# Later modulation vectors on POOL, their weight blocks fetched and added behind fixed units of the projection weights

## The chip, the cores and the metric

The kernel runs on one core of a Trainium2 chip. The metric is the device time of one execution in microseconds (us). TensorE (PE, its weight loads PEld), VectorE (DVE), ScalarE (ACT) and GpSimd (POOL) compute; SyncE (SP) issues all transfers (DMA). Each of them takes its instructions in order and waits for semaphores of the others.

## What is computed

Two layers of a diffusion backbone over 512 latent and 256 context tokens of width 1024. Each layer is modulated: from the vectors c and c_ctx come shift, scale and gate, each as silu(c) @ w_ada[l] + b_ada[l].

```python
for l in range(DEPTH):                                   # 2 layers
    shift, scale, gate = jnp.split(jax.nn.silu(c) @ w_ada[l] + b_ada[l], 3, axis=-1)
    shift_c, scale_c, gate_c = jnp.split(jax.nn.silu(c_ctx) @ w_ada[l] + b_ada[l], 3, axis=-1)
    h = rms_norm(x, norm_g[l]) * (1.0 + scale[:, None]) + shift[:, None]
    hc = rms_norm(ctx, norm_g[l]) * (1.0 + scale_c) + shift_c
    ...  # projections of h and hc by w_in[l]; neighbourhood, latent and differential attention
    x_new = x + gate[:, None] * merge_branches(o_na, o_mla, o_diff, z, gm, w_br[l], w_out[l])
    if not last:
        ctx = ctx + gate_c * merge_branches(co_na, co_mla, co_diff, cz, cgm, w_br[l], w_out[l])
    x = x_new
```

## The kernel before

**Units.** Weights of the projections come as units (`unit`, L133): a load of up to 128x384 float32 into one of seven stages (`ws`), a high half by ACT (L122), and a low half (L127) by DVE or, for every second unit without a gain, by POOL; nine buffers each for `wh` and `wl`. `mm3` (L113) multiplies in three passes (lines 115 to 117).

**Steps.** A layer's `mixer` (L867) runs twelve steps in the order D, M, N (differential, latent, neighbourhood heads), four of each. A step projects its heads (eight units in D and N, four with a gain in M), computes a z gate (three units) and some of the 24 `gm` gates (three units each, their count by `NGM`), and computes the attention of the heads of the step before. Step 0 also holds the compressed projections. Then come the branches, the gate (`ada_gate`, L258) and `out_proj` (L1014), which multiplies its result by the gate and, in layer 0, builds the next layer's h. The framework orders each engine's instructions by priorities (`at`, L80) and by a modelled time line; `issue_after` ties the instructions of one engine in a block behind a given one.

**Modulation vectors.** Each w_ada[l] falls into six chunks of 512 columns: 0 and 1 shift, 2 and 3 scale, 4 and 5 gate; each chunk into eight blocks of 128x512 (256 KB). `ada_rows` (L215) multiplies a block by the two columns silu(c) and silu(c_ctx), as one fp32 matmul (two records) per block into a quarter of the partitions of the one PSUM bank `fl`, which zgate and gm also use. DVE copies the bank to rows (L231). For chunks below 4, `ada_ss` (L244) sums the four quarters and turns the row into columns with four small matmuls (L250), and DVE writes A and B (L254). For the gate chunks, eight rows of 512 go to DRAM (`rowsd`, L242), and `ada_gate` loads them (nine rows with the bias) and spreads them over 128 partitions with a matmul (L270). Four chunks of layer 0 are made at the start (`fast`, tile `fs`); the other eight are later ones (`ada_later`, L233; tile `aw`, four buffers), placed by hand after steps 4, 5, 7, 8, 8 and 10 of layer 0 (chunks 4 and 5 of layer 0, four chunks of layer 1) and after steps 4 and 6 of layer 1 (its chunks 4 and 5).

**POOL** also raises mean squares to the power -0.5 (L167), scales softmax rows of N and M heads (L741), applies parts of the rotary tables (L441, L619 to L635), multiplies outputs by z (L778) and adds branches (L981). PSUM has banks of four kinds: `sc` (one pair), `bk` two, `pj` three, `fl` one.

## Time and profile before

| what | value |
|---|---|
| median of 3 runs | 1945.37 us (1943.38 to 1948.09) |
| the profiled execution | 1946.06 us |
| its span, first to last instruction | 1944.3 us |
| mean granted clock of TensorE | 0.993 |
| PE busy | 1882.9 us |
| DVE, ACT, POOL busy | 1213.2, 936.3, 766.0 us |
| moved by DMA | 243.28 MB |

Busy is the time in which an engine had at least one instruction under way. The ends of matmuls are modelled and overlap, so the start of the next matmul tells more of what one costs than its own length. The granted clock is a share of 2.4 GHz; it has two levels, 1.2 and 2.4 GHz, and a value between is a mean over a stretch.

### The profile page before, as it was taken

Reading aid. Unit: us, or ns where it says so; the run is one execution under the profiler, and the core shown is the slowest. Engines: PE = TensorE matmul, PEld = TensorE weight load, DVE = VectorE, ACT = ScalarE, POOL = GpSimd, SP = SyncE. Lnnn points to the kernel's source line nnn. Section 1 sums busy time; section 2 is a strip of 40 time slices with the busy share of each in tenths; the row PEclk is TensorE's granted clock in tenths of the full one; section 3 lists DMA queues with packets and bytes.
Section 4 is the critical chain, followed back from the end, with each engine's and each line's share of the span. In section 5 each row is a group of like instructions: output and inputs, shape, how many; then the busy total and the mean of one; then the engine's idle time right before and its main releaser. Section 6 shows DMA issues by size and latency. Waiting matters only on the chain.

```text
span 1944.3 us, 33969 instructions
## 1 busy us (share of the span) xinstructions
PE 1882.9 (97%) x11650; PEld 1731.5 (89%) x11650; DVE 1213.2 (62%) x2808; ACT 936.3 (48%) x2422; POOL 766.0 (39%) x1057
## 2 busy tenths in 40 slices
PE   7999999999999999999999999999999999999998
PEld 4999999989998988989899988898799699889878
DVE  5557677746774555646664365667668566766763
ACT  4445456535553544445432254555545446555531
POOL 3434243333532332333356364434344334444363
PEclk9999999999999999999999999999999899999999
DMA  9554123343444333332655243422522422442663
GB/s 319 170 176 144 39 66 112 104 130 115 141 122 131 91 107 123 109 105 80 197 179 171 81 142 123 142 71 79 175 62 73 145 75 84 126 128 65 200 187 117
DMA packets 172600, 243.28 MB, mean 125 GB/s; under 512 B 22710, under 2 KB 127560, under 8 KB 172428
## 3 DMA queue, kind: packets, MB, share of 16 engines
q1 hardware_dynamic: 172428, 241.12, 40.1%
q8 instruction: 92, 1.51, 0.3%
q14 instruction: 80, 0.66, 0.1%
HBM read 190.38 MB, written 44.49 MB: 121 GB/s over the span
## 4 chain that ended last, share of the span: by engine, by line
PE 87%; DVE 4%; DMA 4%; ACT 2%; issue 1%; POOL 1%; SPq 0%; DVEq 0%; ACTq 0%; POOLq 0%
PE pj L117 11%; PE pj L115 11%; PE pj L116 11%; PE fl L115 10%; PE fl L116 9%; PE fl L117 9%; PE sc L690 6%; PE bk L851 4%; PE bk L680 4%; PE fl L230 2%; PE bk L810 2%; PE sc L731 1%; DMA aw<-in_w_ada 1%; PE pj L640 1%; PE pj L451 1%
## 5 line engine op out<-in xcount | busy, mean ns | idle before, releaser
L122 ACT CAST w<-ws 128x384 fp32r<-128x384 f32 (+3 forms) x520 | 236.8, 474 | 260.9 <-PE fl L116 146.7
L127 POOL TENSOR_TENSOR w<-ws,w 128x384 fp32r<-128x384 f32 (+3 forms) x260 | 242.8, 940 | 289.9 <-ACT w L122 279.5
L115 PE MATMUL fl<-h,w 128*128 128x384 f32 (+1 forms) x864 | 313.5, 363 | 4.3 <-DVE zs L392 2.2
L115 PE MATMUL pj<-w,h 128*128 128x384 f32 (+2 forms) x944 | 313.9, 335 | 2.0 <-DVE kl L127 1.1
L116 PE MATMUL pj<-w,h 128*128 128x384 f32 (+2 forms) x944 | 309.7, 329 | 1.1 <-POOL w L127 1.1
L117 PE MATMUL fl<-h,w 128*128 128x384 f32 (+1 forms) x864 | 310.1, 359 | 0.0
L116 PE MATMUL fl<-h,w 128*128 128x384 f32 (+1 forms) x864 | 310.1, 359 | 0.0
L117 PE MATMUL pj<-w,h 128*128 128x384 f32 (+2 forms) x944 | 308.5, 331 | 1.2 <-POOL h L127 1.0
L127 DVE TENSOR_TENSOR w<-ws,w 128x384 fp32r<-128x384 f32 (+2 forms) x260 | 177.5, 687 | 65.5 <-ACT w L122 59.4
L167 POOL TENSOR_TENSOR ss<-ss,nhalf 128x4 f32<-128x4 f32 (+1 forms) x144 | 143.6, 998 | 184.6 <-DVE ss L166 165.5
L741 POOL TENSOR_SCALAR P<-P,st 128x512 f32<-128x512 f32 (+1 forms) x128 | 107.9, 846 | 259.2 <-DVE st L737 223.3
L694 ACT ACTIVATE P<-sc,st 128x768 f32<-128x768 f32 (+1 forms) x192 | 159.5, 832 | 101.5 <-DVE st L775 39.0
L117 PEld LDWEIGHTS pj<-w,h 128*128 128x128 f32 x944 | 177.1, 189 | 10.7 <-issue 5.0
L684 DVE TENSOR_TENSOR pt<-bk,pt 128x512 fp32r<-128x512 f32 (+1 forms) x256 | 147.8, 586 | 61.2 <-ACT pt L683 58.6
L115 PEld LDWEIGHTS pj<-w,h 128*128 128x128 f32 x944 | 177.7, 189 | 9.0 <-issue 4.6
L116 PEld LDWEIGHTS pj<-w,h 128*128 128x128 f32 x944 | 178.4, 189 | 4.1 <-issue 2.5
L115 PEld LDWEIGHTS fl<-h,w 128*128 128x128 f32 x864 | 163.0, 189 | 16.1 <-DVE zs L392 3.7
L683 ACT CAST pt<-bk 128x512 fp32r<-128x512 f32 (+1 forms) x256 | 127.2, 506 | 99.1 <-PE bk L680 96.7
L117 PEld LDWEIGHTS fl<-h,w 128*128 128x128 f32 x864 | 162.8, 188 | 12.1 <-DVE w L127 0.6
L116 PEld LDWEIGHTS fl<-h,w 128*128 128x128 f32 x864 | 163.1, 189 | 9.5
L690 PE MATMUL sc<-qk,qk 96*128 96x512 f32 (+3 forms) x592 | 143.5, 337 | 3.8 <-DMA qk<-qk 2.9
L680 PE MATMUL bk<-cst,P 128*128 128x128 f32 x832 | 130.2, 274 | 4.7 <-DVE pt L684 2.4
(237 smaller groups left out, 3978.3 us busy)
## 6 DMA issues: line engine op xcount, KB each, us to landing
ws<-in_w_qkv SPq DMA_DIRECT2D x128, 192.0 KB
ws<-in_w_gm SPq DMA_DIRECT2D x96, 192.0 KB
aw<-in_w_ada SPq DMA_DIRECT2D x64, 256.0 KB
ct<-cqd SPq DMA_DIRECT2D x40, 384.0 KB
ct<-ckd SPq DMA_DIRECT2D x48, 256.0 KB
ws<-in_w_z SPq DMA_DIRECT2D x48, 192.0 KB
thd<-th SPq DMA_DIRECT2D x48, 192.0 KB
ws<-in_w_br SPq DMA_DIRECT2D x48, 192.0 KB
```

The costliest lines, as they stand in the source:

```text
L115: mm(out, a[0], b[0], start=first, stop=False)
L116: mm(out, a[0], b[1], start=False, stop=False)
L117: mm(out, a[1], b[0], start=False, stop=last)
L122: nc.scalar.copy(hi, src)
L127: (nc.gpsimd if le == "g" else nc.vector).tensor_tensor(lo, src, f(hi), ALU.subtract)
L167: nc.gpsimd.tensor_tensor(out, out, self.nhalf[:, :cols], ALU.pow)
L680: nc.tensor.transpose(pt[:, i * P:(i + 1) * P], src[:, (b0 + i) * P:(b0 + i + 1) * P], self.ident)
L683: nc.scalar.copy(h, v)
L684: nc.vector.tensor_tensor(lo, v, f(h), ALU.subtract)
L690: mm(s[:, d0:d0 + w], x, y, start=i == 0, stop=i == len(ops) - 1)
L694: nc.scalar.activation(p, src, AF.Exp, bias=st[:, m:m + 1], accum_out=st[:, 2 + m:3 + m])
L741: nc.gpsimd.tensor_scalar(p, p, st[:, 4 + m:5 + m], 0.0, ALU.mult, ALU.add)
```

## The change

The eight later vectors are no longer matmuls. `ada_later` only puts their 64 blocks on a list, all of a layer's at step 0. From then on `unit` fetches a block behind the load of every third unit, if no more than one is held (`ada_fetch`; two buffers of `aw` in place of four), and when POOL takes the low half of a unit at least two units later, the block is used behind that (`ada_use`). `ada_add` multiplies the block by silu(c) as a scalar per partition and adds it to an accumulator of 128x512 per stream, both on POOL: two streams for layer 0's chunks and for shift and scale, one for layer 1's gate. After the eighth block, chunks below 4 are summed over partitions by eight matmuls with a column of ones; the gate chunks go to DRAM as 128x512 accumulators, and `ada_gate` loads them, adds the bias to their first row and sums over partitions with a matrix of ones. What is left at the end of the steps is drained.

```diff
-ADA = ((4, 5, 7, 8, 8, 10), (4, 6))
...
+        self.ada_todo, self.ada_held, self.nunit = [], [], 0
+    RATE = 3
...
         self.background(self.last)
+        self.ada_fetch(self.last)
...
             self.nsplit += 1
-            self.split(hi[:, :m], lo[:, :m], raw[:, :m], "a", "g" if self.nsplit % self.NS == 0 else "v")
+            le = "g" if self.nsplit % self.NS == 0 else "v"
+            done = self.split(hi[:, :m], lo[:, :m], raw[:, :m], "a", le)
+            if le == "g":
+                self.ada_use(done)
...
+        self.sC = self.cpool.tile([P, KT, 2], F32, name="sC")
+        nc.vector.tensor_scalar(self.sC, th, 0.5, None, ALU.mult)
+        self.sT = pool.tile([P, KT, 32], F32, name="sT")
...
-                st = self.wpool.tile([P, 512], F32, tag="aw", bufs=4, name=self.n("aw"))
-            if self.AFT and not fast:
-                with self.tc.issue_after(self.last.ins):
-                    nc.sync.dma_start(st, w[:, k])
-            else:
-                nc.sync.dma_start(st, w[:, k])
+                raise AssertionError
+            nc.sync.dma_start(st, w[:, k])
             g = 32 * (k % 4)
             nc.tensor.matmul(ps[g:g + 32, :], self.sT[:, k, :], st, start=k < 4, stop=k >= 4, tile_position=(0, g))
         nc.vector.tensor_copy(rows, ps)
 
     def ada_later(self, l, ch, pool):
-        rows = pool.tile([P, 512], F32, tag="th", bufs=1, name=self.n("arow"))
-        self.ada_rows(l, ch, rows, None, False)
+        self.ada_todo += [(l, ch, k, pool) for k in range(KT)]
+
+    def ada_fetch(self, ins):
+        self.nunit += 1
+        if not self.ada_todo or self.nunit % self.RATE or len(self.ada_held) > 1:
+            return
+        l, ch, k, pool = self.ada_todo.pop(0)
+        st = self.wpool.tile([P, 512], F32, tag="aw", bufs=2, name=self.n("aw"))
+        with self.tc.issue_after(ins.ins):
+            self.nc.sync.dma_start(st, self.io["w_ada"][l, ch][:, k])
+        self.ada_held.append((self.nunit, st, l, ch, k, pool))
+
+    def ada_use(self, ins):
+        if not self.ada_held or self.nunit < self.ada_held[0][0] + 2:
+            return
+        _, st, l, ch, k, pool = self.ada_held.pop(0)
+        with self.tc.issue_after(ins.ins):
+            self.ada_add(st, l, ch, k, pool)
+
+    def ada_drain(self):
+        while self.ada_held or self.ada_todo:
+            if not self.ada_held:
+                l, ch, k, pool = self.ada_todo.pop(0)
+                st = self.wpool.tile([P, 512], F32, tag="aw", bufs=2, name=self.n("aw"))
+                self.nc.sync.dma_start(st, self.io["w_ada"][l, ch][:, k])
+                self.ada_held.append((0, st, l, ch, k, pool))
+            _, st, l, ch, k, pool = self.ada_held.pop(0)
+            self.ada_add(st, l, ch, k, pool)
+
+    def ada_add(self, st, l, ch, k, pool):
+        nc = self.nc
+        strs = (0, 1) if l == 0 or ch < 4 else (0,)
+        if k == 0:
+            self.acc = pool.tile([P, 2, 512], F32, tag="acc", bufs=1, name=self.n("acc"))
+        acc = self.acc
+        for s in strs:
+            g = self.sC[:, k, s:s + 1]
+            if k == 0:
+                nc.gpsimd.tensor_scalar(acc[:, s], st, g, 0.0, ALU.mult, ALU.add)
+                continue
+            t = st
+            if s != strs[-1]:
+                t = self.wpool.tile([P, 512], F32, tag="at", bufs=1, name=self.n("at"))
+            nc.gpsimd.tensor_scalar(t, st, g, 0.0, ALU.mult, ALU.add)
+            nc.gpsimd.tensor_tensor(acc[:, s], acc[:, s], t, ALU.add)
+        if k < KT - 1:
+            return
         if ch < 4:
-            self.ada_ss(l, ch, rows, self.fl())
+            pt = self.fl()
+            for i in range(4):
+                for s in strs:
+                    nc.tensor.matmul(pt[:, 2 * i + s:2 * i + s + 1], acc[:, s, i * P:(i + 1) * P], self.ones[:, 0:1], start=True, stop=True)
+            self.ada_put(l, ch, pt)
             return
         if l not in self.rowsd:
-            self.rowsd[l] = self.dram.tile([2, 4, 2, 512], F32, name=f"rowsd{l}")
-        for g in range(4):
-            self.nc.sync.dma_start(self.rowsd[l][ch - 4, g], rows[32 * g:32 * g + 2, :])
+            self.rowsd[l] = self.dram.tile([2, 2, P, 512], F32, name=f"rowsd{l}")
+        for s in strs:
+            nc.sync.dma_start(self.rowsd[l][ch - 4, s], acc[:, s])
 
     def ada_ss(self, l, ch, rows, pt):
...
+        sel = self.cst[:, C_SEL:C_SEL + 2]
+        for i in range(4):
+            self.nc.tensor.matmul(pt[:, 2 * i:2 * i + 2], rows[:, i * P:(i + 1) * P], sel, start=True, stop=True)
+        self.ada_put(l, ch, pt)
+
+    def ada_put(self, l, ch, pt):
...
-        selb = pool.tile([9, 2, P], F32, tag="selb", bufs=1, name=f"selb{l}")
-        nc.sync.dma_start(selb, self.io["selb"])
         for hf in range(2):
-            rows = pool.tile([9, 512], F32, tag="arow", bufs=1, name=self.n("arow"))
-            nc.sync.dma_start(rows[0:8, :], self.rowsd[l][hf].rearrange("g s n -> (g s) n"))
-            nc.sync.dma_start(rows[8:9, :], self.io["b_gate"][l:l + 1, hf * 512:(hf + 1) * 512])
+            bias = pool.tile([1, 512], F32, tag="gbias", bufs=1, name=self.n("gbias"))
+            nc.sync.dma_start(bias, self.io["b_gate"][l:l + 1, hf * 512:(hf + 1) * 512])
             for s in strs:
+                rows = pool.tile([P, 512], F32, tag="arow", bufs=1, name=self.n("arow"))
+                nc.sync.dma_start(rows, self.rowsd[l][hf, s])
+                nc.vector.tensor_tensor(rows[0:1, :], rows[0:1, :], bias, ALU.add)
                 ps = self.bk()
-                nc.tensor.matmul(ps, selb[:, s, :], rows[0:9, :], start=True, stop=True)
+                nc.tensor.matmul(ps, self.ones, rows, start=True, stop=True)
...
-            for _ in range(ADA[l].count(step)):
-                self.at("ada")
-                self.ada_later(*ada.pop(0), pool)
+            if step == 0:
+                while ada:
+                    self.ada_later(*ada.pop(0), pool)
             self.base += self.PRI["step"]
+        self.ada_drain()
```

The constant `selb` goes, the padded `sT` moves into the pool of the start, and `ada_put` is the rest of the old `ada_ss`.

## Rows read from the trace of the kernel before

**Rows 1.** The page, busy us (share of the span) xinstructions of each engine.

```profile
PE 1882.9 (97%) x11650; PEld 1731.5 (89%) x11650; DVE 1213.2 (62%) x2808; ACT 936.3 (48%) x2422; POOL 766.0 (39%) x1057
```

**Rows 2.** Waits of PE and PEld: waiter, releaser, us in total, times, longest.

```profile
PE fl L230 <- DMA aw<-in_w_ada: 5.8, 5, 3.2
PE pj L451 <- DVE qn L445: 5.3, 5, 1.3
...
PE pj L116 <- POOL w L127: 1.1, 1, 1.1
...
PEld bk L680 <- POOL P L741: 2.7, 3, 1.2
```

**Rows 3.** Groups by form, whole span: busy us, mean ns, idle before.

```profile
L230 PE MATMUL fl<-aw,sT 128*32 128x512 f32 x128 | 40.5, 626 | 5.9 <-DMA aw<-in_w_ada 5.8 <-DVE qn L445 0.2
```

**Rows 4.** Timeline of PE, 477 to 487: start us, us, instruction, count.

```profile
477.07 1.07 PE L230 MATMUL fl<-aw,sT 128*32 128x512 f32 x8
...
484.94 0.34 PE L117 MATMUL pj<-w,h 128*128 128x384 f32 x1
485.21 1.05 PE L230 MATMUL fl<-aw,sT 128*32 128x512 f32 x2
486.19 0.45 PE L115 MATMUL pj<-w,h 128*128 128x384 f32 x1
486.47 0.33 PE L116 MATMUL pj<-w,h 128*128 128x384 f32 x1
```

**Rows 5.** Windows: us, PE, PEld, DVE, ACT, POOL busy, clock, DMA share, GB/s.

```profile
1507.00:1525.00 18.00, 13.58 (x59) 7.73 (x60) 7.40 (x20) 5.85 (x17) 2.38 (x4) 0.72 0.44 131
```

**Rows 6.** Timeline of the same stretch, SP's fetches and PE's wait.

```profile
1509.37 1.83 SPq L228 DMA_DIRECT2D aw<-in_w_ada  x4
...
1514.11 1.91 PE L230 MATMUL fl<-aw,sT 128*32 128x512 f32 x2 [3.15 <-DMA aw<-in_w_ada]
```

**Rows 7.** The chain of waits, start: start us, us, what.

```profile
24.33 1.07 PE fl L250 x8
```

**Rows 8.** Timeline near the end, layer 1's second gate rows.

```profile
1893.59 0.29 SPq L266 DMA_DIRECT2D arow<-rowsd  x1
...
1899.48 1.12 PE L270 MATMUL bk<-arow,selb 9*128 9x512 f32 x2 [0.66 <-DMA arow<-rowsd]
```

**Rows 9.** Groups by form of POOL, 128x512 multiply and add.

```profile
L741 POOL TENSOR_SCALAR P<-P,st 128x512 f32<-128x512 f32 x64 | 49.3, 775 | 73.0 <-DVE st L737 69.2 <-PE bk L720 2.7 <-PE bk L680 0.8
...
L981 POOL TENSOR_TENSOR yf<-yf,tht 128x512 f32<-128x512 f32 x16 | 24.0, 1509 | 6.8 <-DVE tht L980 6.7
```

**Rows 10.** Windows of the two stretches, columns as in rows 5.

```profile
122.00:840.00 718.00, 706.88 (x4555) 668.25 (x4554) 456.82 (x1120) 360.78 (x968) 250.48 (x363) 1.00 0.38 114
1190.00:1400.00 210.00, 200.68 (x1220) 177.12 (x1219) 145.17 (x361) 115.23 (x301) 89.56 (x134) 0.99 0.39 116
```

**Rows 11.** The same windows, POOL busy with L167 alone.

```profile
122.00:840.00 718.00, 64.73 (x62) 1.00 0.38 114
1190.00:1400.00 210.00, 23.65 (x25) 0.99 0.39 116
```

**Rows 12.** The same windows, POOL busy with L741 alone.

```profile
122.00:840.00 718.00, 40.24 (x48) 1.00 0.38 114
1190.00:1400.00 210.00, 13.60 (x16) 0.99 0.39 116
```

**Rows 13.** Waits of SP's queue: waiter, releaser, total, times, longest.

```profile
SPq L228 <- PE fl L230: 57.7, 31, 9.2
```

**Rows 14.** Timeline of DVE splits, POOL idle (1507) and working (1893).

```profile
1507.06 0.55 DVE L127 TENSOR_TENSOR w<-ws,w 128x384 fp32r<-128x384 f32 x1
...
1893.31 1.20 POOL L127 TENSOR_TENSOR w<-ws,w 128x256 fp32r<-128x256 f32 x1
...
1893.82 1.09 DVE L127 TENSOR_TENSOR w<-ws,w 128x384 fp32r<-128x384 f32 x1
```

**Rows 15.** Groups by form, DVE's splits of 128x384.

```profile
L127 DVE TENSOR_TENSOR w<-ws,w 128x384 fp32r<-128x384 f32 x208 | 149.0, 720 | 62.4 <-ACT w L122 57.3 <-PE bk L680 2.0 <-PE fl L117 1.3
```

More of the change, by code (lines that the diff above doesn't have):

```diff
@@ L126, in split @@
             nc.gpsimd.tensor_scalar(hi, src, 1.0, 0.0, ALU.mult, ALU.add)
-        (nc.gpsimd if le == "g" else nc.vector).tensor_tensor(lo, src, f(hi), ALU.subtract)
+        return (nc.gpsimd if le == "g" else nc.vector).tensor_tensor(lo, src, f(hi), ALU.subtract)
     def gsplit(self, hi, lo, src, g):
@@ L144, in unit @@
                 nc.scalar.activation(hi[:, sl], raw[:, sl], AF.Copy, scale=gain[:, i:i + 1])
-                nc.vector.scalar_tensor_tensor(lo[:, sl], raw[:, sl], gain[:, i:i + 1], f(hi[:, sl]), ALU.mult, ALU.subtract)
+                done = nc.vector.scalar_tensor_tensor(lo[:, sl], raw[:, sl], gain[:, i:i + 1], f(hi[:, sl]), ALU.mult, ALU.subtract)
         else:
             self.nsplit += 1
-            self.split(hi[:, :m], lo[:, :m], raw[:, :m], "a", "g" if self.nsplit % self.NS == 0 else "v")
+            le = "g" if self.nsplit % self.NS == 0 else "v"
+            done = self.split(hi[:, :m], lo[:, :m], raw[:, :m], "a", le)
+            if le == "g":
+                self.ada_use(done)
         return [w[:, :m].rearrange("p (a b) -> p a b", a=a) for w in (hi, lo)]
@@ L167, in rstd, with setup @@
         nc.gpsimd.tensor_tensor(out, out, self.nhalf[:, :cols], ALU.pow)
-    def setup(self):
+    def setup(self, pool):
         nc, io = self.nc, self.io
@@ L176, in setup @@
         nc.vector.scalar_tensor_tensor(th, th, 1.0, cc, ALU.add, ALU.mult)
-        self.sT = self.cpool.tile([P, KT, 32], F32, name="sT")
+        self.sC = self.cpool.tile([P, KT, 2], F32, name="sC")
+        nc.vector.tensor_scalar(self.sC, th, 0.5, None, ALU.mult)
+        self.sT = pool.tile([P, KT, 32], F32, name="sT")
         nc.gpsimd.memset(self.sT, 0.0)
@@ L247, in ada_ss @@
         part, hf = ch // 2, ch % 2
-        sel = self.cst[:, C_SEL:C_SEL + 2]
-        for i in range(4):
-            nc.tensor.matmul(pt[:, 2 * i:2 * i + 2], rows[:, i * P:(i + 1) * P], sel, start=True, stop=True)
         v = pt[:, 0:8].rearrange("p (k s) -> p k s", s=2)
@@ L1053, in run @@
         with tc.tile_pool(name="start", bufs=1, reuse_waits="tile") as sp:
-            self.setup()
+            self.setup(sp)
             self.hT_alloc(0)
@@ L1099, in _consts @@
     c[:, C_ONE:C_ONE + P] = 1.0
-    selb = np.zeros((9, 2, P), np.float32)
-    selb[8] = 1.0
     for s in range(2):
         c[s::32, C_SEL + s] = 1.0
-        selb[s:8:2, s] = 1.0
     rope = np.zeros((P, S_N), np.float32)
@@ L1115, in _consts @@
             rope[:, off:off + 4 * dim] = full.reshape(P, 4 * dim)
-    return c, selb, rope
+    return c, rope
 def _layout(np, i):
@@ L1121, in _layout @@
     o = {}
-    o["cst"], o["selb"], o["rope"] = _consts(np)
+    o["cst"], o["rope"] = _consts(np)
     o["x"] = a["x"][0].reshape(8, 64, D).transpose(1, 0, 2).reshape(SEQ, D)
```

## Prediction

> **What bounds the kernel now.** I read the page's busy shares first: PE is busy 97% of the span, DVE 62%, ACT 48%, POOL 39% [rows 1]. Next come PE's waits. A kernel bound by PE shows short ones, each with another releaser, and so it is: the longest that comes back is 5.8 us for `aw`, the blocks of `w_ada`; next is `qn`, 5.3 us, a DVE step right behind POOL's power; POOL itself releases PE or its weight loads for a few us [rows 2]. So work that leaves PE's queue is worth its own length as long as the rest still comes in time. The change takes such work out and puts it on POOL. Three questions follow: how much PE time goes, what new PE work and waits come, and what a fuller POOL does to the chains that pass through it.
>
> **What leaves PE.** Eight later vectors of eight blocks, 64 blocks, two records each: 128 matmuls, busy 40.5 us [rows 3]. Busy time understates them. In the timeline one block stands as 1.05 us, but the two ordinary matmuls around it (L117 at 484.94, then L115, L116) come at 486.19 and 486.47; without it they would follow at the usual 0.17 us, at 485.11 and 485.28. So it displaces 486.47 - 485.28 = 1.19 us. Four blocks that start together share one such place (eight records in 1.07 us) [rows 4]. 40.5 / 1.05 = 38.6 places, x 1.19 = 45.9 us. The waits for `aw` go with them, 5.8 us [rows 2]. In the last vector, 1507 to 1525, the granted clock is 0.72 on average, so part of it ran at 1.2 GHz [rows 5]; PE had waited 3.15 us for a block fetched only at 1509.4, and then a pair of records takes 1.91 instead of 1.05 us [rows 6]. At 0.72 about 56% of the 18 us is at the low level; that share of 13.58 us busy, halved, is 3.8 us, of which I take 2.5, since some of it is waiting of other origin. Together 54.2 us. The eight DVE copies of the rows and the small `rowsd` DMAs go too; they are beside PE and I count nothing.
>
> **What comes onto PE.** For the four later vectors with `ch` < 4, eight matmuls replace four. The old four (eight records) take 1.07 us [rows 7]; the new ones have the same stationary shape and one moving column instead of two, so 4 x 1.07 = +4.3 us. They wait for the last add; behind them in PE's queue stand ordinary projections, and a POOL add that is late by its own length costs at most four times 1.5 us (0 to 6; I take 0, since the fl bank that the old blocks held from the first to the last is now theirs for 1 us only). The gate matmuls stay six, with 128 rows in place of nine: the same columns, nothing.
>
> **The gate at the end.** The old rows are 16 KB and a bias row; the new ones are 256 KB per stream, with one DVE add, in one buffer. In layer 0, four in a row instead of two; out_proj has other tiles to multiply meanwhile (0 to 6 us). In layer 1 it is near the end: the second row load is issued at 1893.59 and PE waits 0.66 us for it at 1899.48 [rows 8]; that is 5.9 us after its issue. A larger load and a DVE add behind it can come later by a few us. Bounds 0 and 6 us, I take 3, half-way, because the out_proj tiles cover part of it.
>
> **What comes onto POOL.** The nearest rows are L741 for the multiply (128x512, 0.775 us) and L981 for the add (128x512, 1.509 us) [rows 9]. A vector with two streams has 16 multiplies and 14 adds: 12.4 + 21.1 = 33.5 us; one with one stream half. Six and two of them: 201 + 33.5 = 235 us, so POOL goes from 766 to about 1000 us, still far below PE. Where does it fall? Blocks are fetched at every third unit from step 1 on. Steps 1 to 11 of layer 0 have 174 units (8 of a D or N projection, 4 of an M one, 3 of each z and gm); 48 blocks need 144, so until roughly 790 us; layer 1's 16 need 48 units, about 1190 to 1400. In 122 to 840 POOL is busy 250 of 718 us (35%), in the second stretch 90 of 210 (43%) [rows 10]. The first goes to 35 + 201/670 = 65%, the second to 59%.
>
> The requests on POOL that a PE transpose waits for are the power of the norms (62 and 25 in the two stretches, L167) and the softmax scaling (48 and 16, L741) [rows 11, 12]: 151. Each meets a block under way about 3 times in 10 and then waits half of a burst of 2 x (0.775 + 1.509) = 4.57 us: 151 x 0.3 x 2.3 = 104 us of delay at those places. How much reaches PE? Today these requests take 142 us of POOL themselves, and the waits of PE and its weight loads that POOL ends, or the DVE step right behind it, are 5.3 + 1.1 + 2.7 = 9.1 us [rows 2]: 6.4%. That share of 104 is 7 us, my value; the bounds are 0 (projections of the next step fill in) and all 104.
>
> The lo halves of the units come later too, but nine buffers stand between them and PE, and PE waited 1.1 us for them in all [rows 2].
>
> **The SP queue.** The same 64 fetches move from one place per vector to one behind every third unit, and two buffers replace four. A fetch waits until POOL has added the block before last, which is placed behind the lo half of a unit three or four back. While it waits, the loads of the following units, the copies of k (`qk`), `ct` and the stores of `th` stand behind it. Today fetches hold SP for 57.7 us in 31 waits on PE [rows 13], so the queue already moves at the pace of free buffers and PE hardly feels it. I count nothing, with the early loads of seven stages as cover; what it costs without them is a rival below. The fetch itself is then early: two units pass before the add. The gate accumulators' way out and in, twelve transfers of 256 KB, lies beside other work.
>
> **Sum** against the profiled execution, 1946.1 us: -45.9 - 5.8 - 2.5 + 4.3 + 3 + 7 = -39.9, so 1906; the median of the runs is 0.7 us lower, which changes nothing.
>
> **The rivals.**
> POOL sets the end (slower). For: power and scaling wait in order behind the adds, and an N or M projection holds its pj bank until the power is there. Against: three pj banks, three P buffers, and only 6% of these requests' time reaches PE today. Net of everything else the saving is 54.2 - 7.3 = 47 us, so it decides from 47/104 = 45% exposed; at 60% the time is 1946 + 15 = 1961, at 100% 2003. 16%.
> The fetch blocks SP. For: in-order queue, two buffers. Price: if in each of the 12 D and N steps of the two stretches the copy of k comes one such wait (57.7/31 = 1.9 us) late, +23 us: 1930. Against: buffers are freed three units ahead. 12%.
> Layer 1 keeps its time. Two of the eight vectors lie where PE lacked other work (the clock fell in the second [rows 5]); freed time there could turn into waiting. 6/8 of 54 us is 41, so 1921. 12%.
> DVE pays. A DVE split of 128x384 takes 0.55 us with POOL idle and 1.09 us while POOL works from 1893.31 on [rows 14]. The mean of 0.72 us over 208 such splits [rows 15] puts the excess at 35 us for 766 us of POOL work, so 235 more add 11 us of DVE time: 1918 if all of it reached PE. 8%.
> By the Trainium skill (SBUF — State Buffer, Who interferes with whom), a DVE instruction with two SBUF inputs and a GpSimd one that reads SBUF exclude each other for the whole instruction; the trace agrees, 1.09 for 0.55 us.
> That the blocks are not spread at all but left for the drain at the end of the steps: 174 units for 144 speak against it; it is in the tails.
>
> **How the numbers follow.** The forecast, 1906, has 52%, its own range 1895 to 1921. Low end of the whole: no give-back, 1946.1 - 54.2 + 4.3 = 1896, and a few us more where layer 1 loses idle time: 1890. The high end takes in the rivals on the faster side: 1945; about 5% lie below and 15% above. A measurement tells about 0.2%, 4 us, from no change. Slower by that: the first rival, 16%. Within: the upper ends of the SP and layer 1 cases, 7%. Faster: 77%.
>
> **What would show it.** L230 with `aw` gone, PE busy down by 35 to 45 us at an unchanged busy share; POOL near 1000 us, its new multiplies and adds near 0.78 and 1.5 us; no dip of the clock near 1510; PE's waits behind L167 and L741 at some 16 us in all. If PE's idle time grows by more than 47 us with POOL steps as releasers, the first rival holds; if `qk` or `ws` loads release PE, the second; if idle time in layer 1 stays while PE work there falls, the third.

## The result and the profile after

The kernel after takes 1975.55 us (1971.98 to 1977.83, 4 runs) where the kernel before took 1946 beside it: 1.0139 times as long, 95% interval 1.0123 to 1.0155. The change makes it slower; 1906 us had been forecast, and the time lies above the whole range.

The page's busy line of after, and then the core's span with its mean granted clock:

```profile
PE 1880.8 (95%) x11554; PEld 1760.0 (89%) x11554; DVE 1248.7 (63%) x2807; ACT 936.9 (47%) x2422; POOL 987.3 (50%) x1267
```

```profile
core 0: 1976.0 us, clock 0.979
```

Against [rows 1], POOL is 221 us busier, as forecast (1000), and DVE 35 us, where the rival "DVE pays" had 11. PE, which loses 128 matmuls of 40.5 us [rows 3] and gains 32 records, is only 2 us less busy, and its idle time goes from 1944.3 - 1882.9 = 61 us to 1976.0 - 1880.8 = 95. The clock says why the busy time stays: 0.993 before means that 2 x 0.007 x 1944 = 27 us ran at 1.2 GHz; 0.979 now means 2 x 0.021 x 1976 = 83 us.

Groups by form (line, engine, operation, tiles, shape, count, busy us, mean ns, idle before): the sums on POOL, and the small matmuls behind them.

```profile
L281 POOL TENSOR_TENSOR acc<-acc,aw 128x512 f32<-128x512 f32 x56 | 75.5, 1348 | 2.0
L281 POOL TENSOR_TENSOR acc<-acc,at 128x512 f32<-128x512 f32 x42 | 55.2, 1315 | 1.2
L280 POOL TENSOR_SCALAR aw<-aw,sC 128x512 f32<-128x512 f32 x56 | 43.7, 781 | 0.2
L280 POOL TENSOR_SCALAR at<-aw,sC 128x512 f32<-128x512 f32 x42 | 33.0, 786 | 7.9 <-DMA aw<-in_w_ada 7.9
L275 POOL TENSOR_SCALAR acc<-aw,sC 128x512 f32<-128x512 f32 x14 | 10.8, 783 | 0.1
...
L288 PE MATMUL fl<-cst,acc 128*128 128x1 f32 x64 | 7.7, 244 | 1.3 <-POOL acc L281 1.3
```

The sums take 218 us of POOL where 235 were estimated; a multiply is as in [rows 9], an add shorter (1.35 against 1.509 us). PE waits 1.3 us for a sum in the whole run. So the estimate of POOL's work held; what it does to others did not.

PE's waits of after (waiter, releaser, total, times, longest), without those at the start:

```profile
PE sc L745 <- ACT P L749: 7.7, 7, 2.5
PE bk L735 <- POOL P L796: 7.5, 5, 2.6
PE fl L116 <- DVE zs L447: 7.4, 8, 1.7
PE pj L506 <- DVE qn L500: 6.8, 7, 1.5
PE bk L735 <- DVE u L910: 4.2, 3, 2.5
PE bk L906 <- DVE pt L739: 4.0, 4, 2.5
...
PE fl L118 <- DVE w L128: 3.3, 1, 3.3
...
PE fl L118 <- POOL w L128: 2.1, 2, 1.5
...
PE pj L117 <- POOL w L128: 1.2, 1, 1.2
```

Beside [rows 2], the waits for `aw` are gone, `qn` went from 5.3 to 6.8, and POOL's scaled softmax rows from 2.7 (weight loads) to 7.5. But most of the new idle time has other releasers, DVE and ACT, in steps that the change leaves as they were: summed over the lines of the view, the waits that DVE ends go from 35.8 to 56.4 us, those of ACT from 8.3 to 16.2, those of POOL from 2.1 to 13.1, and those of the DMA from 9.4 to 3.9. The timeline shows how one arises (start us, us, engine, instruction, [idle before]):

```profile
739.36 1.47 POOL L281 TENSOR_TENSOR acc<-acc,at 128x512 f32<-128x512 f32 x1
...
739.94 1.17 DVE L491 TENSOR_TENSOR qn<-qn,rows 128x256 f32<-128x256 f32 x1
...
740.79 1.44 POOL L281 TENSOR_TENSOR acc<-acc,aw 128x512 f32<-128x512 f32 x1
741.04 1.22 DVE L171 TENSOR_SCALAR ss<-ss 128x4 f32<-128x4 f32 x1
742.17 0.68 DVE L739 TENSOR_TENSOR pt<-bk,pt 128x512 fp32r<-128x512 f32 x1
...
742.91 0.86 PE L906 MATMUL bk<-pt,V 128*128 128x256 f32 x4 [2.51 <-DVE pt L739]
...
743.70 0.15 DVE L171 TENSOR_SCALAR ss<-ss 128x4 f32<-128x4 f32 x1
```

DVE's step of 128x4 elements takes 0.15 us at 743.70, and 1.22 us at 741.04: it ends at 742.26, when POOL's add ends (742.23). The step before it, which took 0.42 us at 739.28, took 1.17 beside the add before. `pt` stands in order behind it on DVE, and PE waits 2.51 us for `pt`. What follows costs a second time. Windows (us, then busy us of PE, PEld, DVE, ACT and POOL with counts, clock, DMA share, GB/s):

```profile
740.00:744.00 4.00, 1.49 (x11) 1.26 (x10) 4.00 (x8) 1.35 (x3) 3.32 (x4) 0.92 0.31 99
744.00:748.00 4.00, 4.00 (x21) 4.00 (x21) 0.93 (x3) 0.37 (x1) 1.05 (x1) 0.50 0.08 30
748.00:752.00 4.00, 4.00 (x19) 4.00 (x18) 0.43 (x1) 0.36 (x1) 0.73 (x1) 0.73 0.09 33
```

PE was busy 1.49 of 4 us, and the next 4 us run at 0.50, the lower level, with PE busy throughout. By the Trainium skill (SBUF — State Buffer, Who interferes with whom), DVE and GpSimd share a pair of ports, and for a DVE step that needs the pair, as a `tensor_scalar` can, whichever has it first keeps it for its whole instruction; the trace agrees, 1.22 for 0.15 us. My rival "DVE pays" had priced this from the splits alone, which barely changed (738 ns after, 720 in [rows 15]); I had overlooked the small steps. They are a part of it: against e1_no_add (below), DVE is 39 us busier, of which the 128x4 step has 8.4 and these splits 8.3.

### The profile page after: what moved, and what is told of

It reads as the page before. It is cut to its first block, busy times and chain, and to the rows that moved or that the text cites. A ratio compares the mean times of both kernels' runs of the same rounds, so it can differ in the third digit from the quotient of the medians.

```text
span 1976.0 us, 33984 instructions
## 1 busy us (share of the span) xinstructions
PE 1880.8 (95%) x11554; PEld 1760.0 (89%) x11554; DVE 1248.7 (63%) x2807; ACT 936.9 (47%) x2422; POOL 987.3 (50%) x1267
## 3 DMA queue, kind: packets, MB, share of 16 engines
q8 instruction: 91, 1.49, 0.3%
## 4 chain that ended last, share of the span: by engine, by line
PE 83%; DVE 7%; ACT 3%; POOL 3%; issue 2%; DMA 2%; SPq 0%; ACTq 0%; DVEq 0%; POOLq 0%
PE pj L116 11%; PE pj L118 11%; PE pj L117 11%; PE fl L116 9%; PE fl L117 9%; PE fl L118 9%; PE sc L745 6%; PE bk L906 5%; PE bk L735 4%; PE bk L865 2%; PE sc L786 1%; DVE w L128 1%; PE pj L695 1%; PE pj L506 1%; POOL w L128 1%
## 5 line engine op out<-in xcount | busy, mean ns | idle before, releaser
L116 PE MATMUL fl<-h,w 128*128 128x384 f32 (+1 forms) x864 | 318.2, 368 | 11.2 <-DVE zs L447 7.4
L116 PE MATMUL pj<-w,h 128*128 128x384 f32 (+2 forms) x944 | 318.7, 340 | 2.0 <-DVE kl L128 1.1
L118 PE MATMUL fl<-h,w 128*128 128x384 f32 (+1 forms) x864 | 313.3, 363 | 5.4 <-DVE w L128 3.3
L117 PE MATMUL pj<-w,h 128*128 128x384 f32 (+2 forms) x944 | 313.2, 333 | 1.2 <-POOL w L128 1.2
L117 PE MATMUL fl<-h,w 128*128 128x384 f32 (+1 forms) x864 | 313.2, 362 | 0.0
L118 PE MATMUL pj<-w,h 128*128 128x384 f32 (+2 forms) x944 | 312.3, 334 | 0.4 <-POOL h L128 0.2
L128 DVE TENSOR_TENSOR w<-ws,w 128x384 fp32r<-128x384 f32 (+2 forms) x260 | 182.4, 704 | 56.7 <-ACT w L123 53.1
L116 PEld LDWEIGHTS fl<-h,w 128*128 128x128 f32 x864 | 165.5, 192 | 25.9 <-DVE zs L447 9.6
L116 PEld LDWEIGHTS pj<-w,h 128*128 128x128 f32 x944 | 180.6, 192 | 6.9 <-ACT h L399 2.7
L118 PEld LDWEIGHTS pj<-w,h 128*128 128x128 f32 x944 | 179.1, 191 | 4.7 <-DVE h L401 2.3
L117 PEld LDWEIGHTS pj<-w,h 128*128 128x128 f32 x944 | 181.3, 192 | 1.7 <-POOL w L128 1.4
L118 PEld LDWEIGHTS fl<-h,w 128*128 128x128 f32 x864 | 165.1, 191 | 18.6 <-DVE w L128 3.7
L117 PEld LDWEIGHTS fl<-h,w 128*128 128x128 f32 x864 | 165.5, 192 | 9.9
L745 PE MATMUL sc<-qk,qk 96*128 96x512 f32 (+3 forms) x592 | 145.4, 341 | 11.7 <-ACT P L749 7.7
```

Source lines behind the costliest of these rows:

```text
L116: mm(out, a[0], b[0], start=first, stop=False)
L117: mm(out, a[0], b[1], start=False, stop=False)
L118: mm(out, a[1], b[0], start=False, stop=last)
L128: return (nc.gpsimd if le == "g" else nc.vector).tensor_tensor(lo, src, f(hi), ALU.subtract)
L745: mm(s[:, d0:d0 + w], x, y, start=i == 0, stop=i == len(ops) - 1)
```

## Experiments

Microseconds are given as (ratio - 1) x 1946, since each ratio compares with runs of before on the same chip. An interval is 3 to 8 us to either side, so differences of a few us between two kernels are not told apart.

| kernel | median us | ratio [95%] | us against before |
|---|---|---|---|
| after | 1975.55 | 1.0139 [1.0123, 1.0155] | +27.1 |
| e6_none | 1922.72 | 0.9861 [0.9837, 0.9884] | -27.1 |
| e3_half_pe | 1927.71 | 0.9898 [0.9870, 0.9926] | -19.9 |
| e9_double_pe | 1972.63 | 1.0144 [1.0119, 1.0170] | +28.0 |
| p1_packs | 1929.59 | 0.9897 [0.9869, 0.9925] | -20.0 |
| e7_bare | 1939.49 | 0.9945 [0.9924, 0.9965] | -10.7 |
| e10_gate | 1921.38 | 0.9878 [0.9855, 0.9902] | -23.7 |
| e12_no_pool | 1937.30 | 0.9948 [0.9928, 0.9969] | -10.1 |
| e14_no_small | 1921.84 | 0.9874 [0.9847, 0.9901] | -24.5 |
| e1_no_add | 1942.21 | 0.9979 [0.9965, 0.9993] | -4.1 |
| e2_no_fetch | 1967.59 | 1.0101 [1.0075, 1.0127] | +19.7 |
| e5_write_only | 1948.45 | 1.0005 [0.9991, 1.0020] | +1.0 |
| e8_long_fills | 1960.61 | 1.0076 [1.0049, 1.0104] | +14.8 |
| e13_long_reads | 1959.15 | 1.0055 [1.0035, 1.0076] | +10.7 |
| e15_two_reads | 1973.66 | 1.0147 [1.0107, 1.0188] | +28.6 |
| e11_halves | 1975.03 | 1.0162 [1.0129, 1.0195] | +31.5 |
| e4_dve | 1964.52 | 1.0088 [1.0058, 1.0118] | +17.1 |

### Adds or fetches?

e1_no_add keeps the fetches and replaces the sums by one element; e2_no_fetch keeps the sums and fetches one block once (every product then goes to `at`, so that this block stays as it is).

```diff
 # e1_no_add
...
-            nc.gpsimd.tensor_scalar(t, st, g, 0.0, ALU.mult, ALU.add)
-            nc.gpsimd.tensor_tensor(acc[:, s], acc[:, s], t, ALU.add)
+            nc.gpsimd.tensor_scalar(acc[:, s, k:k + 1], st[:, k:k + 1], g, 0.0, ALU.mult, ALU.add)
 # e2_no_fetch
...
-            self.nc.sync.dma_start(st, self.io["w_ada"][l, ch][:, k])
+        if not hasattr(self, "aw0"):
+            self.aw0 = self.cpool.tile([P, 512], F32, name="aw0")
+            self.nc.sync.dma_start(self.aw0, self.io["w_ada"][l, ch][:, k])
+        st = self.aw0
...
-            if s != strs[-1]:
+            if True:
                 t = self.wpool.tile([P, 512], F32, tag="at", bufs=1, name=self.n("at"))
```

> The changed kernel with the multiply and add of blocks 1 to 7 of each vector left out on POOL (one 128x1 multiply per block and stream stays, so the sums are not formed); fetches, buffers, their places and the small matmuls stay. Theory A (POOL's long instructions, through its queue or by holding up DVE, open gaps on PE, and the clock falls in them): 1900 to 1920 us, PE idle back near 60 us, time at the low clock back near 25 us. Theory B (the fetches hold SP): 1955 to 1980. Theory C (the planner's other order of PE, whatever POOL does): 1940 to 1980.

> The changed kernel with the 64 fetches left out: every block is the same resident tile, loaded once, so the sums are not those of the weights; all multiplies and adds on POOL stay in their places. Theory A: 1965 to 1985 us, as the changed kernel. Theory B: 1900 to 1930. Theory C: anything from 1950 to 1990.

The sums are worth 27.1 + 4.1 = 31.2 us, the fetches 27.1 - 19.7 = 7.4. So the sums outweigh the fetches by four to one. Theory A has the larger part right, but not that without the sums the time falls to 1920 us or less; 1942 us lies in the range of theory C alone. e1's busy line, and its span and clock:

```profile
PE 1864.9 (96%) x11554; PEld 1749.5 (90%) x11554; DVE 1209.6 (62%) x2807; ACT 934.7 (48%) x2422; POOL 814.3 (42%) x1169
```

```profile
core 0: 1940.5 us, clock 0.986
```

PE runs the same 11554 instructions as in after, in a partly different order, and is 15.9 us less busy; at the lower level it spends 2 x 0.014 x 1940.5 = 54 us instead of 83. Half of the 29 us between them is 14.5, which is about the 15.9. The other part is idle time, 95.2 against 75.6 us. But without any sums e1 is only 4 us below before: the saving on PE is missing too.

### What the matmuls were worth

```diff
 # e6_none (before without the later vectors)
-        self.ada_rows(l, ch, rows, None, False)
+        self.nc.vector.memset(rows, 0.0)
 # e3_half_pe (before, blocks 0 to 3 only)
-            else:
+            elif fast or k < 4:
                 nc.sync.dma_start(st, w[:, k])
...
-            nc.tensor.matmul(ps[g:g + 32, :], self.sT[:, k, :], st, start=k < 4, stop=k >= 4, tile_position=(0, g))
+            if fast or k < 4:
+                nc.tensor.matmul(ps[g:g + 32, :], self.sT[:, k, :], st, start=k < 4, stop=k >= 4 or not fast, tile_position=(0, g))
 # e9_double_pe (before, a second matmul per later block)
...
+            if not fast:
+                nc.tensor.matmul(ps[g:g + 32, :], self.sT[:, k, :], st, start=False, stop=k >= 4, tile_position=(0, g))
```

> The kernel before with the eight later vectors left out altogether: no fetch, no matmul on PE, a fill in place of the copied row; the small matmuls and the gate stay. What all that PE work is worth by itself. By the account of the prediction 1946 - 54 = 1892 to 1900 us; by the rate of the run with half of it left out (19.3 us for 30 of 38.6 places) 1918 to 1926.

> The kernel before with blocks 4 to 7 of each later vector left out (32 fetches and 32 matmuls on PE, the ones that stand singly; the sums are not complete); nothing is added anywhere. What PE work removed is worth by itself: 30 places of 1.19 us and the waits for blocks, so 1900 to 1912 us if PE time is worth its length (theory A and B); 1930 to 1960 if a changed order eats it (theory C).

> The kernel before with the matmul of each later block issued twice (the sums are doubled); 64 more of the matmuls that the change removes, and nothing else. If one place on PE costs its 1.19 us: +45 us, 1992. If PE time here is worth what taking it away gave (24 us for all): +20 to +27, 1967 to 1974. A larger slope up than down means that the waits of other chains lie below the work that was removed.

Without any of the later vectors 27.1 us are saved, half of the 54.2 of the prediction; without half the blocks 19.9; doubled, they cost 28.0. By the groups 40.5 us of matmul records leave in e6_none, 30.1 in e3_half_pe (10.4 left), and 35.1 are added in e9_double_pe (75.6 in all). That is 0.67, 0.66 and 0.80 us of time for a microsecond of records. The page of e6_none and two of its waits say where a part of the rest went:

```profile
PE 1849.7 (96%) x11522; PEld 1731.9 (90%) x11522; DVE 1206.5 (63%) x2808; ACT 937.3 (49%) x2422; POOL 771.0 (40%) x1057
```

```profile
PE fl L115 <- DVE zs L392: 7.6, 9, 2.8
PE sc L731 <- ACT P L694: 4.2, 5, 1.8
```

PE's busy time falls by 33.2, and its idle time does not fall by the 5.8 us of `aw` but rises from 61.4 to 73.0. In the trace of before PE waits 2.2 us for `zs` and 0.9 for this `P`. The likely reading is that the block matmuls lay where DVE and ACT were about to be late, and covered them; since the order of PE's other work differs too (more on this below), it is not shown.

p1_packs computes everything and keeps the matmuls on PE, but fetches four blocks at once, so that four start together.

```diff
-                st = self.wpool.tile([P, 512], F32, tag="aw", bufs=4, name=self.n("aw"))
+                if k % 4 == 0:
+                    pk = self.wpool.tile([P, 4, 512], F32, tag="aw", bufs=1, name=self.n("aw"))
+                    nc.sync.dma_start(pk, w[:, k:k + 4])
+                st = pk[:, k % 4]
...
-            else:
+            elif fast:
                 nc.sync.dma_start(st, w[:, k])
```

> The kernel before with the later vectors kept on PE, but four blocks fetched by one transfer of 1 MB into one buffer of four, twice per vector, so that the four matmuls start together on the four quarters: 16 places of 1.19 us in place of 38.6. By the prediction's account -27 us, so 1920; at the rate of the run with half left out -14 us, 1933; if the load of 1 MB comes too late for the second four, 1945 to 1955.

```profile
L233 PE MATMUL fl<-aw,sT 128*32 128x512 f32 x128 | 17.9, 633 | 4.2 <-DMA aw<-in_w_ada 4.2
```

The same 128 records take 17.9 instead of 40.5 us [rows 3], as the four in one place of [rows 4] promised, and 20.0 us are saved. This is faster than before and after; it comes within about 7 us of having no later vectors at all.

### What the change costs without sums and fetches

e7_bare has neither; e12_no_pool also leaves POOL out (DVE fills the accumulators), e14_no_small the small matmuls as well. e10_gate is e6_none with the new gate loads.

```diff
 # e7_bare: e2_no_fetch with the sum of e1_no_add
 # e12_no_pool: e7_bare with
-            nc.gpsimd.tensor_scalar(acc[:, s, k:k + 1], st[:, k:k + 1], g, 0.0, ALU.mult, ALU.add)
...
-                nc.gpsimd.tensor_scalar(acc[:, s], st, g, 0.0, ALU.mult, ALU.add)
+                nc.vector.memset(acc[:, s], 0.0)
 # e14_no_small: e12_no_pool with
-            for i in range(4):
-                for s in strs:
-                    nc.tensor.matmul(pt[:, 2 * i + s:2 * i + s + 1], acc[:, s, i * P:(i + 1) * P], self.ones[:, 0:1], start=True, stop=True)
+            nc.vector.memset(pt[:, 0:8], 0.0)
 # e10_gate: e6_none with
...
-            rows = pool.tile([9, 512], F32, tag="arow", bufs=1, name=self.n("arow"))
-            nc.sync.dma_start(rows[0:8, :], self.rowsd[l][hf].rearrange("g s n -> (g s) n"))
...
+                rows = pool.tile([P, 512], F32, tag="arow", bufs=1, name=self.n("arow"))
+                nc.sync.dma_start(rows, self.io["w_ada"][l, 4 + hf][:, s])
+                nc.vector.tensor_tensor(rows[0:1, :], rows[0:1, :], bias, ALU.add)
```

> The changed kernel without fetches and without the adds of blocks 1 to 7 (a 128x1 multiply of a resident tile stays in each place, so the sums are not formed). What remains of the change: accumulators, eight small matmuls, larger gate rows, the start, and the planner's order. If fetches cost 8 us and adds 33 us independently: 1934 us. If the order of PE alone costs what is missing (theory C): well above the kernel without any later vectors, by 10 us or more.

> The kernel without any later vectors (1922.7 us), with the changed kernel's gate: row tiles of 128x512 loaded one after the other into one buffer (blocks of w_ada stand in for the accumulators), the bias added by DVE, a matrix of ones. The changed kernel without fetches and adds took 1939.5, 17 us more. If the gate's loads are most of that: 1930 to 1936. By the prediction's term (3 us): 1923 to 1928. The rest is then the eight small matmuls (4 us) and the order.

> The bare change of e7_bare (no fetches, no sums), with POOL's 98 one-element multiplications and its 14 products of block 0 left out as well (DVE fills the accumulators instead); the four to eight small matmuls of each chunk, the stores of the accumulators and the gate's loads stay. e7_bare stood at 1939.5 us and the kernel without any later vectors (e6_none) at 1922.7; open is what the 16.8 us between them are. Theory 'POOL's queue': its instructions behind the splits, about 41 us of POOL's busy time there, cost 10 us or more: 1923 to 1930 us. Rival 'the small matmuls and the order of the work': 1936 to 1942 us.

> The kernel of e12_no_pool with the small matmuls of the chunks left out too (DVE fills their eight elements of PSUM instead), so that of the change only the stores of the accumulators, the gate's loads and the earlier place of the modulation's last steps are left. Theory 'the small matmuls cost what was estimated for them, 4 us': 3 to 6 us below e12_no_pool. Rival 'they cost nothing, the rest is order': within 2 us of e12_no_pool. If e12_no_pool already stands at 1930 us or less, both give 1922 to 1930 us here.

The bare change stands 16.4 us above e6_none, where 7.3 had been estimated for small matmuls and gate. The gate loads are 3.4 us, not told apart from 0 nor from the 3 estimated. POOL's small instructions are nothing (e12_no_pool 0.6 us above e7_bare). Taking the small matmuls out gives 24.5 - 10.1 = 14.4 us (the two intervals leave about 7.5 to 21). PE in e12_no_pool and in e14_no_small:

```profile
PE 1860.4 (96%) x11554; PEld 1746.8 (90%) x11554; DVE 1215.7 (63%) x2821; ACT 937.2 (48%) x2422; POOL 771.1 (40%) x1057
```

```profile
PE 1850.9 (96%) x11490; PEld 1735.1 (90%) x11490; DVE 1213.6 (63%) x2825; ACT 937.3 (49%) x2422; POOL 769.2 (40%) x1057
```

64 records less are 9.5 us of busy time and, from the spans of 1933.8 and 1918.2 us, 6.1 of idle. Neither of my two expectations, 3 to 6 us and nothing, held. In e12_no_pool the group of line 284 has 7.7 us and no wait ahead of it; why they cost twice that is open. The order of the work differs here as well, and its share is not known. Like with like, eight small matmuls per vector against the old four with the same gate, is e12_no_pool against e10_gate: 23.7 - 10.1 = 13.6 us (about 6 to 21). Against e6_none, which has 32 such records of the old kind, e14_no_small is level.

e1_no_add against e7_bare is the fetches a second time: 10.7 - 4.1 = 6.6 us, beside the 7.4 above. And e2_no_fetch against e7_bare is the sums a second time: 19.7 + 10.7 = 30.4 us, beside the 31.2.

### What it is in POOL's work

Four kernels have e1's one-element step and, in place of the 98 sums of blocks 1 to 7, POOL work of about the same total (the sums took 207 us).

```diff
 # e5_write_only
...
+            t = self.wpool.tile([P, 512], F32, tag="at", bufs=1, name=self.n("at"))
+            for _ in range(4):
+                nc.gpsimd.memset(t, 0.0)
 # e8_long_fills
...
+            for _ in range(2):
+                nc.gpsimd.memset(acc, 0.0)
 # e13_long_reads
...
+            for _ in range(2):
+                nc.gpsimd.tensor_scalar(acc[:, :, 0:384], acc[:, :, 0:384], 1.0, 0.0, ALU.mult, ALU.add)
 # e15_two_reads
...
+            for _ in range(2):
+                nc.gpsimd.tensor_tensor(acc[:, s, 0:352], acc[:, 0, 0:352], acc[:, 1, 0:352], ALU.add)
```

> The changed kernel with each multiply and add of blocks 1 to 7 replaced by the 128x1 multiply and four fills of 128x512 on POOL, which write and read nothing (the sums are not formed); 392 fills. It tells POOL's queue from its reads. If the changed kernel loses by DVE steps that stand still while POOL reads two operands (theory A1): near the kernel without adds, 1942 to 1952 us, with DVE's small steps (128x4) back at 0.24 us. If it loses by what queues on POOL (A2): 1942 plus 33 us times the ratio of the fills' length to the 2.0 us of a multiply and an add; at equal length some 1975.

> The changed kernel with each multiply and add of blocks 1 to 7 replaced by the 128x1 multiply and two fills of the accumulator (128x1024) on POOL, so fewer and longer instructions that only write (the sums are not formed). The run with four short fills kept POOL as busy as the adds do and came to 1948 us. If what counts is that the adds read SBUF beside DVE: 1945 to 1955 us again. If what counts is the length of one POOL instruction (1.3 us of an add against 0.53 of a fill): 1965 to 1980.

> The kernel after with the sums left out as in e8_long_fills (blocks 1 to 7 are not added), but each of the two long fills of an accumulator is now an in-place multiplication of 768 of its 1024 elements in each partition, which reads and writes them (the width is set so that one should take about 1.0 us, near the 0.955 us of the fill; 196 of them in both kernels). Theory 'reading is what holds DVE': DVE's 128x4 step at line 171 goes from the 278 ns of e8 to 290 ns or more, and the time to 1970 to 1980 us. Rival 'only POOL's time and the length of its instructions count': the time stays at that of e8, 1957 to 1966 us, scaled by any difference in POOL's busy time (988.7 us in e8). A third case, that an operation with two operands in SBUF (the adds of the kernel after) is what costs: the time stays near e8 while DVE's steps are no longer than there.

> The kernel of e13_long_reads (sums left out, 196 long POOL operations in place of them), but each long operation is a sum of two operands in SBUF of 128x352 elements instead of a multiplication of one operand of 128x768 in place (0.864 us there); by the 1.26 us that the sum of 128x512 takes in the kernel after, one should take 0.85 to 0.95 us, so that POOL is as busy as there. Theory 'a POOL operation that reads two operands holds DVE, one that reads a single operand does not': DVE's 128x4 step at line 171 goes from the 252 ns of e13 to 290 ns or more, DVE's total above 1245 us, and the time to 1968 us or more (1959.15 in e13). Rival 'the number of operands doesn't matter': 1955 to 1963 us with DVE's step near 252 ns; what the kernel after loses beyond that would then lie in the fetched tile that its sums hold.

The groups of these operations, in this order:

```profile
L280 POOL MEMSET at<- 128x512 f32 x392 | 206.4, 527 | 13.8
```

```profile
L279 POOL MEMSET acc<- 128x1024 f32 x196 | 187.2, 955 | 7.5
```

```profile
L281 POOL TENSOR_SCALAR acc<-acc 128x768 f32<-128x768 f32 x196 | 169.4, 864 | 11.2
```

```profile
L281 POOL TENSOR_TENSOR acc<-acc 128x352 f32<-128x352 f32 x196 | 191.5, 977 | 10.4
```

Above e1_no_add they cost 5.1, 18.9, 14.8 and 32.7 us. So a busier POOL is not by itself what costs: 206 us of short fills are worth 5.1, where the estimate for all of POOL's work was 7. Longer instructions cost 15 to 19, whether they fill or read one operand. Two operands in the same count and about the same length cost 17.9 more (e13 to e15, about 9 to 27 by the two intervals; of it some 2 us may go to POOL's 23 us more work, at e13's own price of 14.8 us for 165), and that is the whole of what after loses (31.2).

It does not follow that the operands are the cause, because none of these edits changes POOL's work alone: the framework orders each engine's instructions by a modelled time line, and the order moves with each of them. In e13_long_reads and e15_two_reads PE's instructions stand in the same order up to the 881st, and of all 11554 only 9604 can be put in one common order; for after and e1_no_add it is 9480. What an order is worth by itself was not measured. The price of the sums, found twice in four different orders (31.2 and 30.4), is hardly an accident of order. The step from one operand to two rests on a single pair.

The traces do show which DVE steps POOL holds up. By the Trainium skill (SBUF — State Buffer, Who interferes with whom), a GpSimd instruction that only writes SBUF leaves a two-input DVE instruction alone and one that reads it does not, with no word on the number of operands read. The traces agree: DVE's splits of 128x384, which have two inputs, take 0.55 us in the mean where only fills run beside them (16 cases, 0.56 at most), as with POOL idle; where only one-operand products run beside them it is 0.84 (6 cases), and with two-operand sums 1.08 (5). The 128x4 step, with one input, is held by all three kinds, here in e8_long_fills, e13_long_reads and e15_two_reads:

```profile
252.09 0.96 POOL L279 MEMSET acc<- 128x1024 f32 x1
252.19 0.89 DVE L171 TENSOR_SCALAR ss<-ss 128x4 f32<-128x4 f32 x1
```

```profile
256.86 0.83 POOL L281 TENSOR_SCALAR acc<-acc 128x768 f32<-128x768 f32 x1
257.01 0.71 DVE L171 TENSOR_SCALAR ss<-ss 128x4 f32<-128x4 f32 x1
```

```profile
308.80 1.02 POOL L281 TENSOR_TENSOR acc<-acc 128x352 f32<-128x352 f32 x1
308.93 0.91 DVE L171 TENSOR_SCALAR ss<-ss 128x4 f32<-128x4 f32 x1
```

With POOL idle throughout, this step takes 0.17 us at most. Those that last over 0.5 us all end within 0.05 us of the end of a POOL instruction, and there are 11 of 120 in before already, 16, 15 and 14 in these three, and 17 in after. Its group in before, e5_write_only, e8_long_fills, e13_long_reads, e15_two_reads and after:

```profile
L166 DVE TENSOR_SCALAR ss<-ss 128x4 f32<-128x4 f32 x120 | 28.3, 236 | 2.1
```

```profile
L171 DVE TENSOR_SCALAR ss<-ss 128x4 f32<-128x4 f32 x120 | 31.1, 260 | 2.2
```

```profile
L171 DVE TENSOR_SCALAR ss<-ss 128x4 f32<-128x4 f32 x120 | 33.3, 278 | 1.9
```

```profile
L171 DVE TENSOR_SCALAR ss<-ss 128x4 f32<-128x4 f32 x120 | 30.2, 252 | 1.9
```

```profile
L171 DVE TENSOR_SCALAR ss<-ss 128x4 f32<-128x4 f32 x120 | 31.5, 263 | 2.0
```

```profile
L171 DVE TENSOR_SCALAR ss<-ss 128x4 f32<-128x4 f32 x120 | 35.5, 296 | 1.9
```

The mean of this step does not follow the time: it is longer in e8_long_fills than in e15_two_reads, which is 13.8 us slower. So of the expectation for e15_two_reads the time came true, but its reason, that one operand does not hold DVE and two do, did not: the step has 263 ns instead of 290 or more, and DVE's total rises only from 1237.0 to 1243.4 us. In the two profiled runs PE is equally busy (1874.2 and 1873.8 us), and its idle time goes from 84.3 to 95.2. Of these 10.9 us, 6.8 are waits that POOL's own steps end (3.9 to 10.7, summed over the view's lines), most of it in two, in e13_long_reads and in e15_two_reads:

```profile
PE pj L695 <- POOL qn L690: 2.1, 2, 1.2
...
PE bk L735 <- POOL P L796: 0.5, 1, 0.5
```

```profile
PE pj L695 <- POOL qn L690: 4.6, 3, 2.4
PE bk L735 <- POOL P L796: 4.5, 3, 2.6
```

The wait for `P` is 3.9 us in e1_no_add too, which has no sums, so the order of the work may well be its reason. What it is in the sums that costs 31 us stays open, then: that a held DVE step can open a gap on PE is shown in single places, like the one at 741, and its share in the sum is not.

Two ways to soften it, both computing everything: e11_halves cuts each sum into two of 256 columns, e4_dve does them fused on DVE.

```diff
 # e11_halves
...
+            for c in (slice(0, 256), slice(256, 512)):
+                nc.gpsimd.tensor_scalar(t[:, c], st[:, c], g, 0.0, ALU.mult, ALU.add)
+                nc.gpsimd.tensor_tensor(acc[:, s, c], acc[:, s, c], t[:, c], ALU.add)
 # e4_dve
...
+            nc.vector.scalar_tensor_tensor(acc[:, s], st, g, acc[:, s], ALU.mult, ALU.add)
```

> The changed kernel with every multiply and add of blocks 1 to 7 cut into two halves of 128x256, so POOL reads as much in instructions half as long (392 in place of 196). If DVE's short steps wait for the end of one reading POOL instruction, each wait is halved: 1950 to 1968 us, in spite of a longer POOL time. If the sum of reading time counts, or the queue: 1976 to 1995.

> The changed kernel with the sums on DVE: one fused multiply-add of 128x512 per block and stream (112 instructions, some 0.65 to 0.7 us each, 75 us in all) behind DVE's low halves, in place of 210 instructions on POOL. Theory A, if it is POOL's long instructions: 1900 to 1925 us. If any such work in front of DVE's short steps costs as much: 1940 to 1970. Theory B: 1960 to 1980.

The halves change nothing that can be told: the adds take 771 ns instead of 1.35 us, but POOL is 1026.9 us busy, 40 more. If DVE's waits for the end of one POOL instruction were what costs, half the length should have given 1950 to 1968 us; it did not. On DVE the sums are 98 instructions of 873 ns and 6.6 us of first products, 89 us in place of POOL's 218, and the time is 10 us better than after, yet 17 worse than before, as expected if any such work in front of DVE's short steps costs (1940 to 1970): the waits of PE that DVE ends sum to 69.7 us there and to 56.4 in after.

## Why the prediction was wrong

Its sum was -54.2 + 4.3 + 3 + 0 + 7 = -39.9. The runs give -27.1 (e6_none) + 16.4 (e7_bare) + 6.6 (fetches) + 31.2 (sums) = +27.1, a chain of kernels each compared with the next. No single term turns the sign: with 7 us for the sums it would be +2.9, with -54.2 for what leaves PE 0.0.

- **What leaves PE**, 54.2, is the first step that failed, by 27 us. The 1.19 us is what one place of the timeline shows, and there are 36 places in PE's order where 38.6 were estimated; but "worth its own length as long as the rest still comes in time" was taken as fulfilled because no wait of before was long. In e6_none PE's busy time falls by 33.2 us and its idle time rises by 11.6, in waits that [rows 2] cannot show (`zs` 2.2 to 7.6 us); why they come up is argued, not shown. The clock's dip at [rows 5] did go, as said: 1507 to 1545 is at 1.00 in after. But in the whole run the lower level has 83 us in place of 27.
- **What comes onto PE**, 4.3, is 13.6 like with like (e10_gate to e12_no_pool), and leaving all eight small matmuls out gives 14.4. The busy time had been sized about right (7.7 us for all 64 records), its price had not; why is open.
- **The gate**, 3, is 3.4 and not distinguishable from nothing. In after the second gate load of layer 1 goes out at 1924.55 and DVE's add comes at 1931.24, 6.7 us later, but PE has no wait of its own there.
- **The SP queue**, 0, is 7. The queue stands 45.0 us in 26 waits for POOL's sums where it stood 57.7 on PE [rows 13], so these waits did not grow; the rival's `qk` waits went from 2.9 to 3.9 us. By which way the fetches cost 7 us is not shown.
- **What comes onto POOL**, 7, is 31.2, the second step that failed. The term counted one path: a power or a scaling that queues behind a burst of sums. That path was sized about right. The waits behind the two were to be some 16 us, and `qn` 6.8, `P` 7.5 and `w` 2.1 + 1.2 make 17.6; in e1_no_add, without sums, they are 5.1 + 3.9 + 1.1 = 10.1, so the sums add 7.5. What was left out, or put under the rival "DVE pays" at 11 us, is the rest. Between the profiled runs of e1_no_add and after, PE has 19.6 us more idle time and 15.9 us more busy time. In the first, the waits that POOL ends rise by 7.9 us (5.2 to 13.1) and those that DVE ends by 11.7 (44.7 to 56.4); of the second, some 14.5 are the lower clock that the gaps bring, which the sum had at nothing. What in the sums makes DVE late is open.
- **The rival "POOL sets the end"** named the right side, but its mechanism covers only a part. It asked for 47 us of PE waits with POOL's steps as releasers; there are some 18, and POOL is busy 50%. It needed so much because the saving was thought to be 47 net.

## What to carry to other kernels

The worth of taking work from a bound engine is not its records' length: try it by leaving the work out (here 27 of 54 us), before anything is built to replace it. Work moved to POOL is not free while POOL is half idle: look at the smallest DVE steps beside its instructions, fills included, and at what stands behind them in order, and price PE's gaps twice, once as idle time and once by the clock. Where a framework chooses the order of the work, compare the orders of two kernels before their difference is put down to the edit. And look first for a way to let the same work overlap itself where it is: starting four block matmuls together gave 20 us with a few lines.

## What the runs showed of the hardware

- A DVE step of 128x4 elements that takes 0.15 us at 743.70, with no POOL instruction beside it, took 1.22 us beside a POOL add and ended with it; one of 128x2 elements went the same way at 1275.66 (1.14 us, to 1276.80; POOL's add ended at 1276.78). POOL's fills and one-operand products hold such a step as its sums do, as the three pairs of lines above show.

```profile
1275.52 1.26 POOL L281 TENSOR_TENSOR acc<-acc,aw 128x512 f32<-128x512 f32 x1
1275.66 1.14 DVE L876 TENSOR_SCALAR st<-st 128x2 f32<-128x2 f32 x1
```

- POOL's time per element depends on the kind of operation: a fill of 128x1024 takes 0.955 us, a one-operand product of 128x768 in place 0.864, a sum of two operands of 128x352 0.977, so that the sum handles under half as many elements in a microsecond as either.
- Four fp32 matmuls in four quarters of the partitions that start together took 17.9 us for 128 records in 16 places; before, in 36 places, they took 40.5.
